# A hybrid recurrence and attention block on one core: the first value block by seven products, three projection blocks moved ahead of the recurrence, other places in the queues, and shorter shares of a pair

## The chip, the core and the metric

One core of one Trainium2 chip. The metric is device microseconds of one execution; the kernel before takes 1605.4 us, the median of three runs (1603.4 to 1609.9).

The engines are called by the names of the profile: PE is TensorE (PEld its weight loads), DVE is VectorE, ACT is ScalarE, POOL is GpSimd, SP is SyncE, which issues most loads. A "q" behind a name is that engine's queue, where its DMAs are issued.

## The reference, cut to what matters

```python
xn = rmsnorm(h, norm_gain) * (1 + scale) + shift        # 256 tokens; cn: 256 tokens of the context
aq, ak, av, ag, hq, hff, hfb, hi, hg, ma, mb = split_columns(xn @ w_in)      # w_in: 2048 x 19456
caq, cak, cav, cag, chq, chff, chfb, chi, chg, cma, cmb = split_columns(cn @ w_in)
q = rope(aq) * q_scale;  k = rope(ak)
att = window_attention(q, k, av, cak, cav, sink) * silu(ag)
# two gated recurrences over the tokens, forward and backward, 16 heads of 128 x 128,
# that start from the final states of the context
o, _, _ = hgrn2_bidir(to_heads(silu(hq)), to_heads(hi), k_f, g_f, k_b, g_b, s_f, s_b)
hgb = rmsnorm(o) * hgrn_norm_gain * silu(hg)
y = sigmoid(ma + b_merge[0]) * (hgb @ w_o_hgrn) + sigmoid(mb + b_merge[1]) * (att @ w_o_attn)
out = rmsnorm(h + gate * (y @ w_out)) * final_norm_gain
```

Everything is float32. The columns that both x and the context need are `hff` and `hfb` (forget gates), `hi` (values), `ak` and `av`. The others are needed for x alone.

## The kernel before

**Projections.** A float32 matrix product is made of three products of a coarser type: a weight chunk `raw` of 128 x 1024 (512 KB, loaded by SP, five buffers, `wload` L61) is split into `wh` (ACT, a copy, L78) and `wl` (DVE, raw minus wh, L79), three buffers of each; the activations lie split in `xHL`. High by high, low by high and high by low are summed in a PSUM bank (L93, L94, L96). The planner is told to put both halves of a split ahead of nearly everything else on their engines (`high_priority`). `proj_tok_g` (L101) makes 512 output columns for a list of token tiles in eight chunks; for two token tiles (x alone) that is 96 matmuls of 512 columns, for four (x and context) 192. `proj_col_x_g` (L140) makes 256 columns turned, with the weights as the moving or still side, for x alone.

**Seven products.** Where x and context are both wanted, `quad_tok` (L672) and `quad_col` (L624) treat tokens and columns as 2 x 2 blocks and make seven products of half size instead of eight, from sums of the tokens that `token_sums` (L555) makes once (the buffer `S`) and from sums of the weights (`combos`, L596, on DVE). A `quad_tok` of 512 columns is 336 matmuls of 256 columns (L717, L719, L722). Its results go to DRAM by POOL's queue (L727).

**Order of the stages.** (1) Modulation, and the first columns of the forget gates, up to 133 us. (2) The token stage: `proj_tok` of the first 512 value columns for four token tiles (`bv0`, L730); the two `token_sums` are made on DVE and ACT beside it; then `output_gate(0)` for x alone. (3) Three `quad_tok` of values, one of keys and one of attention values, and thirteen `quad_col` of forget gates, up to about 656 us. (4) The recurrence, eight pairs of heads, up to about 1252 us. (5) Attention together with `part_a` (`w_o_hgrn`), then `part_b` (`w_o_attn`), then `w_out`.

**The recurrence.** On PE the order is written by hand (`manual_schedule`): `weave` (L1028) lets `pair` (L781) run up to its next `yield` and then takes as much filler from `inputs` as that yield asks for, in units of 24 x 512 columns (`STEP`). The yields of a pair are its shares: 2.0, 0.5, 1.75, 4.0, 1.25 and 1.25 units. They lie between: turning of the context's forget gates (L919); `sb`, the state from the context (L936); the first levels (L856, after the copies of L829 and L832); the second levels (L856, after the products of L902), then `kt` (L962); `own` (L977), the pair's own contribution to the state; `S2` (L982, DVE), the state after half of the tokens; `ob` (L994 to L996), the output. The filler is the list `blocks` of `side_work` (L1158), 19 blocks of x alone in eight chunks of half a unit each, and at the end of each pair four chunks for the next pair's queries. `SIDE` (L1173) says how many items of the list fall to a pair: 20, the last pair 31. On the other engines the planner sets the order by its own model of time, except where `issue_after` queues an instruction behind a given one of the same engine.

Beside the filler run: `tasks_on` (L1082) at items 7, 10, 13 and 16 of a pair, which turns the attention's keys and queries: `attn_keys` (L1097) loads a tile `kr` from DRAM on POOL's queue, rotates it on DVE (`rope`, L1061, result `kx`) and is turned on PE at the next task (L1092); `load_forgets` (L1147), which loads the next pair's gates `F` by POOL and makes the context's decay by scans on DVE (`ctx_decay`, L765; L774, L778, L779); `gates` (L523), which sums 64 chunks `hgw` of `w_ada` into the output gate of the block, one chunk per 1.25 units of filler: a load of 256 KB into a single buffer (POOL, L526), one DVE instruction (L197), and after each sixteen chunks four transposes (L203). What is left of `gates` at the end is done by `run(gate)` (L1236). The results of the blocks go to DRAM: output gates `hg` (L521), rotated queries `qr` (L1133) and attention gates `ag` (L1145) by POOL's queue, merge gates (L1059) by ACT's. The small tiles `sm` have three buffers, `bb` two.

Of the kernel before, what the change touches and what calls it, by code (L numbers as in the profile page):

```python
# [7 lines left out]
F32 = mybir.dt.float32  # L8
# [30 lines left out]
def block_kernel(ctx: ExitStack, tc: tile.TileContext, x, c, cx, c_ctx, w_ada, b_ada, norm_gain, w_in,  # L39
# [29 lines left out]
    last_lo = [None]  # L69

    def wchunk(w, row0, nk, col0, ncol):
        cl = col0 if isinstance(col0, tuple) else (col0,)
        raw, rv = wload(w, row0, nk, cl, ncol)
        h = wp.tile([P, 1024], F32R, tag="wh", name="wh", bufs=3)
        lo = wp.tile([P, 1024], F32R, tag="wl", name="wl", bufs=3)
        n = len(cl) * nk * ncol
        with tc.high_priority(PRIO):
            act.activation(h[:, :n], raw[:, :n], AF.Copy)  # L78
            last_lo[0] = dve.tensor_tensor(lo[:, :n], raw[:, :n], h[:, :n].bitcast(F32), op=ALU.subtract).ins  # L79
        parts = [(h[:, g * nk * ncol: (g + 1) * nk * ncol].rearrange("p (k c) -> p k c", k=nk),  # L80
                  lo[:, g * nk * ncol: (g + 1) * nk * ncol].rearrange("p (k c) -> p k c", k=nk)) for g in range(len(cl))]
        return parts if isinstance(col0, tuple) else parts[0]
# [463 lines left out]
    with pl("sp", reuse_waits="tile") as sp:  # L546
# [182 lines left out]
        with tc.manual_schedule(engines={mybir.EngineType.PE}):  # L729
            bv0 = proj_tok(w_in, C_HI, x_st, range(4))  # L730
            for g in range(2):
                token_sums(g)
            for t in range(2):
                vo = fp.tile([P, 2, 512], F32, tag="F0", name="vo", bufs=2)
                with tc.high_priority(2 * PRIO):
                    act.activation(vo[:, 0, :], bv0[t], AF.Copy)
                    dve.tensor_copy(vo[:, 1, :], bv0[2 + t])
                nc.gpsimd.dma_start(v_dr[0][t], vo.rearrange("p a c -> p (a c)"))
            run(output_gate(0))
            for g in range(1, 4):  # L740
                quad_tok(C_HI + 512 * g, v_dr[g])
# [6 lines left out]

    def bias_row(row, n, late=None):
        bb = base.tile([P, 512], F32, tag="bb", name="bb", bufs=2)  # L750
        if late is not None:

            pool.tensor_copy(bb[:, 0:1], late)
        nc.gpsimd.dma_start(bb, row_bcast(b_merge[row: row + 1, n * 512: (n + 1) * 512], 512))
        return bb

# [24 lines left out]
    def pair(g, p, F, banks_q):  # L781
# [140 lines left out]
        yield 2.0  # L922
# [21 lines left out]
        yield 1.75  # L944
# [9 lines left out]
        yield 4.0  # L954
# [14 lines left out]
        yield 1.25  # L969
# [14 lines left out]
        yield 1.25  # L984
# [67 lines left out]
    def merge_out(row, n):  # L1052
        bb = bias_row(row, n)
        bm = yield from proj_tok_g(w_in, (C_MA, C_MB)[row] + n * 512, x_st, range(2))
        for t in range(2):
            sg = base.tile([P, 512], F32, tag="sm", name="sgm", bufs=3)
            dve.tensor_tensor(sg, bm[t], bb, op=ALU.add)
            act.activation(sg, sg, AF.Sigmoid)
            nc.scalar.dma_start((ma_dr, mb_dr)[row][n][:, t * 512: (t + 1) * 512], sg)  # L1059

# [19 lines left out]
    tasks, task = [], [None]  # L1080
# [16 lines left out]
    def attn_keys(z, t):  # L1097
        def fetch():
            kr = base.tile([P, 512], F32, tag="sm", name="kr", bufs=3)
            nc.gpsimd.dma_start(kr, kv_dr[0][t][:, z * 512: (z + 1) * 512])  # L1100
            if z == 0:
                kx, kr = kr, base.tile([P, 512], F32, tag="sm", name="kx", bufs=3)
                rope(kr.rearrange("p (r h d) -> p r h d", r=2, h=2), kx, t)
            return lambda: turn_tile(kr, [X[:, z: 8: 2, t * P: (t + 1) * P] for X in (XH, XL)])
        return fetch

    def attn_values():
        for t in range(4):
            vr = base.tile([P, 512], F32, tag="sm", name="vr", bufs=3)
            nc.gpsimd.dma_start(vr, kv_dr[1][t % 2][:, (t // 2) * 512: (t // 2 + 1) * 512])  # L1110
            rows = slice(8 + 2 * t, 10 + 2 * t)
            split(XH[:, rows, :], XL[:, rows, :], vr.rearrange("p (r c) -> p r c", r=2))
            yield

    def attn_queries(j):
# [14 lines left out]
        for t in range(2):  # L1130
            qr = base.tile([P, 512], F32, tag="sm", name="qr", bufs=3)
            rope(qr.rearrange("p (r h d) -> p r h d", r=2, h=2), bq[t], t)
            nc.gpsimd.dma_start(qr_dr[j][:, t * 512: (t + 1) * 512], qr)  # L1133
            tasks.append(lambda t=t: fetch(t))

    def attn_gates(j):
        for hf in range(2):
            bg = yield from proj_col_x_g(w_in, C_G + 512 * j + 256 * hf)
            for i, b in enumerate(bg):
# [5 lines left out]
                nc.gpsimd.dma_start(ag_dr[j][:, c0: c0 + T], sg)  # L1145

    def load_forgets(n):  # L1147
# [5 lines left out]
        for d in range(2):  # L1153
            ctx_decay(F, (d,))
# [3 lines left out]
    def side_work():  # L1158
        values = attn_values()
        tasks.extend(attn_keys(z, t) for z in range(2) for t in range(2))  # L1160
        blocks = (output_gate(1), merge_out(0, 0), output_gate(2), attn_queries(0), merge_out(0, 1), output_gate(3),
# [3 lines left out]
        for n, g in enumerate(blocks):  # L1165
            for k, got in enumerate(g):
                yield got
                if n > 16 and k % 2:
                    next(values, None)
            yield 0  # L1170

    side = side_work()
    SIDE = (20, 20, 20, 20, 20, 20, 20, 31)  # L1173
# [361 lines left out]
```

## Time and profile before

| | us |
|---|---|
| median of the runs (lowest, highest) | 1605.37 (1603.41, 1609.92) |
| the profiled execution | 1600.81 |
| its span, first to last instruction | 1599.0 |
| busy in the span: PE, PEld, DVE, ACT, POOL | 1570.7, 1343.6, 1182.7, 855.4, 157.6 |

The profile is of one execution. The span is what its rows add up to; 1.8 us of the execution lie around it. A PE row's length is partly modelled, so successive matmuls overlap in the rows: the distance between two starts is the pace of PE. `PEclk` is the granted TensorE clock as a share of 2.4 GHz; 0.5 is the lower of its two levels. A wait names the engine that came last before the waiting instruction could start.

### The profile page before, as it was taken

To read this page: it belongs to the slowest core of one execution; us is meant where nothing else is said; L and a number is where in the kernel's file an instruction comes from. 1 tells how busy PE (TensorE), PEld (TensorE's weight loads), DVE (VectorE), ACT (ScalarE), POOL (GpSimd) and SP (SyncE) were. 2 spreads that over 40 slices of the span, in tenths; PEclk is the share of its full clock that TensorE was granted. 3 is DMA by queue.
4 is the path that set the end of the run, shared out by engine and by line. 5 is a ranking of instruction groups with operands and counts; after the bars stand their busy time and mean duration, and the time that the engine had idled before them with its cause. 6 is when DMAs were issued, how large, how long until landed. Compare 5 with 4: busy or idle time off the path is not lost.

```text
span 1599.0 us, 27552 instructions
## 1 busy us (share of the span) xinstructions
PE 1570.7 (98%) x10810; PEld 1343.6 (84%) x10810; DVE 1182.7 (74%) x1745; ACT 855.4 (53%) x1338; POOL 157.6 (10%) x312
## 2 busy tenths in 40 slices
PE   7999999999999999999999999999999999999998
PEld 4567899999888888878888888788888888888887
DVE  4449677777888888786978887887977677757764
ACT  4334343333555555656566566565566776744442
POOL 2000000000000000111122222122112100000000
PEclk9999999999999999999999999999999999999999
DMA  9995533434444444776778787676788754558761
GB/s 368 386 386 175 160 120 127 138 130 129 148 134 132 132 132 132 250 235 219 234 251 282 248 266 240 223 263 218 249 275 277 254 160 157 158 172 281 231 209 69
DMA packets 238290, 333.81 MB, mean 209 GB/s; under 512 B 12080, under 2 KB 155856, under 8 KB 237392
## 3 DMA queue, kind: packets, MB, share of 16 engines
q1 hardware_dynamic: 212048, 249.54, 47.8%
q0 software_dynamic: 21216, 70.38, 12.8%
q10 hardware_dynamic: 4896, 12.13, 2.2%
q8 instruction: 85, 1.39, 0.4%
q14 instruction: 45, 0.37, 0.1%
HBM read 300.53 MB, written 31.47 MB: 208 GB/s over the span
## 4 chain that ended last, share of the span: by engine, by line
PE 90%; DMA 4%; DVE 3%; issue 2%; ACT 1%; SPq 0%; POOL 0%; POOLq 0%; DVEq 0%; ACTq 0%
PE pj L93 13%; PE pj L96 13%; PE pj L94 13%; PE pj L147 7%; PE pm L645 4%; PE pj L150 4%; PE pj L645 3%; PE pj L717 2%; PE pj L722 2%; PE pj L719 2%; PE pm L648 2%; PE pm L717 2%; PE pm L722 2%; PE pm L719 2%; PE pj L648 2%
## 5 line engine op out<-in xcount | busy, mean ns | idle before, releaser
L78 ACT ACTIVATE wh<-raw 128x1024 fp32r<-128x1024 f32 x292 | 307.2, 1059 | 262.3 <-PE pj L94 175.2
L79 DVE TENSOR_TENSOR wl<-raw,wh 128x1024 fp32r<-128x1024 f32 x292 | 354.8, 1222 | 125.3 <-ACT wh L78 121.5
L93 PE MATMUL pj<-wh,xHL 128*128 128x512 f32 (+1 forms) x832 | 326.2, 393 | 0.7 <-ACT sg L212 0.7
L94 PE MATMUL pj<-wh,xHL 128*128 128x512 f32 (+1 forms) x832 | 321.4, 388 | 0.0
L96 PE MATMUL pj<-wl,xHL 128*128 128x512 f32 (+1 forms) x832 | 219.7, 388 | 3.6 <-DVE wl L79 3.6
L93 PEld LDWEIGHTS pj<-wh,xHL 128*128 128x128 f32 x832 | 157.4, 189 | 33.1 <-ACT sg L212 1.9
L96 PEld LDWEIGHTS pj<-wl,xHL 128*128 128x128 f32 x832 | 154.6, 189 | 35.5 <-DVE wl L79 4.0
L94 PEld LDWEIGHTS pj<-wh,xHL 128*128 128x128 f32 x832 | 157.6, 189 | 30.2
L620 ACT ACTIVATE wh<-T 128x1024 fp32r<-128x1024 f32 x69 | 73.2, 1061 | 150.9 <-DVE T L601 75.5
L620 ACT ACTIVATE wh<-raw 128x1024 fp32r<-128x1024 f32 x92 | 96.8, 1054 | 62.2 <-PE pj L719 20.2
L147 PE MATMUL pj<-xHL,wh 128*128 128x512 f32 x512 | 129.9, 395 | 0.0
L621 DVE TENSOR_TENSOR wl<-raw,wh 128x1024 fp32r<-128x1024 f32 x92 | 112.1, 1219 | 7.4 <-ACT wh L620 7.3
L147 PEld LDWEIGHTS pj<-xHL,wh 128*128 128x128 f32 x512 | 92.5, 189 | 16.8
L621 DVE TENSOR_TENSOR wl<-T,wh 128x1024 fp32r<-128x1024 f32 x69 | 84.2, 1221 | 28.8 <-ACT wh L620 28.8
L150 PEld LDWEIGHTS pj<-xHL,wl 128*128 128x128 f32 x512 | 69.9, 190 | 5.5 <-issue 0.5
L150 PE MATMUL pj<-xHL,wl 128*128 128x256 f32 x512 | 71.6, 283 | 0.3 <-issue 0.3
L197 DVE SCALAR_TENSOR_TENSOR acc<-hgw,cg,acc 128x512 f32<-128x512 f32 x60 | 44.9, 749 | 29.6 <-DMA hgw<-in_w_ada_dram 29.5
L902 DVE TENSOR_TENSOR A<-A,X 128x512 f32<-128x512 f32 x96 | 61.9, 687 | 1.5 <-ACT Kmt L832 0.7
L526 POOL DMA_DIRECT2D hgw<-in_w_ada_dram x64 | 34.8, 544 | 263.8 <-DVE acc L197 210.0
L645 PE MATMUL pm<-S,wh 128*128 128x512 f32 x224 | 56.7, 395 | 0.8 <-ACT s L652 0.7
L601 DVE TENSOR_TENSOR T<-raw,T 128x1024 f32<-128x1024 f32 x46 | 56.1, 1219 | 0.0
L601 DVE TENSOR_TENSOR raw<-raw 128x1024 f32<-128x1024 f32 x23 | 28.2, 1225 | 35.3 <-DMA raw<-in_w_in_dram 35.3
(359 smaller groups left out, 3037.9 us busy)
## 6 DMA issues: line engine op xcount, KB each, us to landing
raw<-in_w_in_dram SPq DMA_DIRECT2D x300, 512.0 KB, 4.5
raw<-in_w_ada_dram SPq DMA_DIRECT2D x64, 512.0 KB, 8.0
hgw<-in_w_ada_dram POOLq DMA_DIRECT2D x64, 256.0 KB, 4.4
raw<-in_w_o_hgrn_dram SPq DMA_DIRECT2D x32, 512.0 KB, 3.6
raw<-in_w_o_attn_dram SPq DMA_DIRECT2D x32, 512.0 KB, 4.3
raw<-in_w_out_dram SPq DMA_DIRECT2D x28, 512.0 KB, 3.9
F<-F POOLq DMA_DIRECT2D x16, 512.0 KB, 6.6
F<-F ACTq DMA_DIRECT2D x13, 512.0 KB, 4.4
```

The costliest lines, as they stand in the source:

```text
L78: act.activation(h[:, :n], raw[:, :n], AF.Copy)
L79: last_lo[0] = dve.tensor_tensor(lo[:, :n], raw[:, :n], h[:, :n].bitcast(F32), op=ALU.subtract).ins
L93: pe.matmul(o, s[0], m[0], start=first, stop=False)
L94: pe.matmul(o, s[1], m[0], start=False, stop=False)
L96: pe.matmul(o, s[0], m[1], start=False, stop=last)
L147: pe.matmul(o.rearrange("p (a t) -> p a t", a=2), h[:, j, cs_], xHL[:, :, k0 + j, :T], start=k0 + j == 0, stop=False)
L150: pe.matmul(o[:, :T], lo[:, j, cs_], xH[:, k0 + j, :T], start=False, stop=k0 + j == KT - 1)
L601: dve.tensor_tensor(o, x_, y_, op=ALU.subtract)
L620: act.activation(h, src, AF.Copy)
L621: dve.tensor_tensor(lo, src, h.bitcast(F32), op=ALU.subtract)
L645: pe.matmul(m_[z].rearrange("p (z a t) -> p z a t", z=2, a=2), h[:, k, :], mv(k), start=fresh and k == 0, stop=False, skip_group_check=True)
L648: pe.matmul(pairs_of(m_[z][:, :T]), lo[:, k, :], mv(k)[:, 0], start=False, stop=k == 7, skip_group_check=True)
```

## The change

1. **Token stage.** The first value block is made by `quad_tok` like the other three. Beside the token sums stand `output_gate(0)`, `output_gate(1)`, `output_gate(2)` and `merge_out(0, 0)`, of which the last three leave the recurrence's list.
2. **Places in the queues.** `behind_chunk` queues what is traced within it behind the newest `wh` on ACT and the newest `wl` on DVE. It is put around `ctx_decay`, the rotation of keys, the splits of attention values and the sending of outputs. The rotation of a key tile becomes a task of its own, one after the load. Outputs of `output_gate`, `attn_queries` and `attn_gates` are collected in `outs` and sent by `send` on ACT's queue, in the recurrence one chunk later.
3. **Shares.** A pair's yields become 1.75, 0.5, 1.5, 3.5, 1.0 and 1.0 units, `SIDE` 17 for a pair and 25 for the last, for a list of 16 blocks. The pace of `gates` stays one chunk per 1.25 units.

```diff
-    last_lo = [None]
+    last_hi, last_lo = [None], [None]
+
+    def behind_chunk():
+        both = ExitStack()
+        both.enter_context(tc.issue_after(last_hi[0]))
+        both.enter_context(tc.issue_after(last_lo[0]))
+        return both
...
-            act.activation(h[:, :n], raw[:, :n], AF.Copy)
+            last_hi[0] = act.activation(h[:, :n], raw[:, :n], AF.Copy).ins
...
+    outs, tasks, task = [], [], [None]
+
+    def send():
+        while outs:
+            o = outs.pop(0)
+            nc.scalar.dma_start(*o[:2])
+            tasks.extend(o[2:])
...
-            nc.gpsimd.dma_start(hg_dr[g][:, t * 512: (t + 1) * 512], sg)
+            outs.append((hg_dr[g][:, t * 512: (t + 1) * 512], sg))
...
-            bv0 = proj_tok(w_in, C_HI, x_st, range(4))
-            for g in range(2):
-                token_sums(g)
-            for t in range(2):
-                vo = fp.tile([P, 2, 512], F32, tag="F0", name="vo", bufs=2)
-                with tc.high_priority(2 * PRIO):
-                    act.activation(vo[:, 0, :], bv0[t], AF.Copy)
-                    dve.tensor_copy(vo[:, 1, :], bv0[2 + t])
-                nc.gpsimd.dma_start(v_dr[0][t], vo.rearrange("p a c -> p (a c)"))
-            run(output_gate(0))
-            for g in range(1, 4):
+            for n, g in enumerate((output_gate(0), output_gate(1), output_gate(2), merge_out(0, 0))):
+                run(g)
+                send()
+                if n < 2:
+                    token_sums(n)
+            for g in range(4):
                 quad_tok(C_HI + 512 * g, v_dr[g])
...
-        yield 2.0
+        yield 1.75
...
-        yield 1.75
+        yield 1.5
...
-        yield 4.0
+        yield 3.5
...
-        yield 1.25
+        yield 1.0
...
-        yield 1.25
+        yield 1.0
...
-        if task[0]:
-            task[0]()
-        task[0] = tasks.pop(0)() if tasks else None
+        task[0] = (task[0]() if task[0] else None) or (tasks.pop(0)() if tasks else None)
...
-            if z == 0:
-                kx, kr = kr, base.tile([P, 512], F32, tag="sm", name="kx", bufs=3)
-                rope(kr.rearrange("p (r h d) -> p r h d", r=2, h=2), kx, t)
-            return lambda: turn_tile(kr, [X[:, z: 8: 2, t * P: (t + 1) * P] for X in (XH, XL)])
+            dst = [X[:, z: 8: 2, t * P: (t + 1) * P] for X in (XH, XL)]
+            if z:
+                return lambda: turn_tile(kr, dst)
+
+            def rotate():
+                kx = base.tile([P, 512], F32, tag="sm", name="kx", bufs=3)
+                with behind_chunk():
+                    rope(kx.rearrange("p (r h d) -> p r h d", r=2, h=2), kr, t)
+                return lambda: turn_tile(kx, dst)
+            return rotate
...
-            nc.gpsimd.dma_start(qr_dr[j][:, t * 512: (t + 1) * 512], qr)
-            tasks.append(lambda t=t: fetch(t))
+            outs.append((qr_dr[j][:, t * 512: (t + 1) * 512], qr, lambda t=t: fetch(t)))
...
-                nc.gpsimd.dma_start(ag_dr[j][:, c0: c0 + T], sg)
+                outs.append((ag_dr[j][:, c0: c0 + T], sg))
...
-            ctx_decay(F, (d,))
+            with behind_chunk() if last_lo[0] else ExitStack():
+                ctx_decay(F, (d,))
...
-        blocks = (output_gate(1), merge_out(0, 0), output_gate(2), attn_queries(0), merge_out(0, 1), output_gate(3),
+        blocks = (attn_queries(0), merge_out(0, 1), output_gate(3),
...
                 yield got
-                if n > 16 and k % 2:
+                if outs and k == 0:
+                    with behind_chunk():
+                        send()
+                if n > NB - 3:
                     next(values, None)
             yield 0
+        send()
...
-    SIDE = (20, 20, 20, 20, 20, 20, 20, 31)
+    SIDE = (17, 17, 17, 17, 17, 17, 17, 25)
```

## Rows read from the trace of the kernel before

**Rows 1.** The page: busy time of TensorE; the chain that ended last, by engine.
```profile
PE 1570.7 (98%) x10810; PEld 1343.6 (84%) x10810; DVE 1182.7 (74%) x1745; ACT 855.4 (53%) x1338; POOL 157.6 (10%) x312
...
PE 90%; DMA 4%; DVE 3%; issue 2%; ACT 1%; SPq 0%; POOL 0%; POOLq 0%; DVEq 0%; ACTq 0%
```

**Rows 2.** Waits of engine PE: us in total, times, longest us.
```profile
PE tkt L1092 <- DVE kx L1072: 3.9, 1, 3.9
PE pj L96 <- DVE wl L79: 3.6, 1, 3.6
```

**Rows 3.** Windows: length, then busy us (instructions) per engine, PEclk, DMA, GB/s.
```profile
132.70:199.50 66.80, 66.09 (x289) 53.76 (x289) 53.33 (x50) 28.81 (x32) 2.70 (x5) 1.00 0.48 157
...
177.60:199.50 21.90, 21.89 (x97) 18.02 (x97) 13.12 (x12) 7.91 (x8) 1.06 (x2) 1.00 0.67 214
199.58:239.90 40.32, 40.32 (x338) 40.31 (x337) 30.48 (x30) 16.53 (x18) 1.63 (x3) 1.00 0.37 120
```

**Rows 4.** Timeline of DVE in the first pair: start us, us, instruction, idle before.
```profile
706.23 0.69 DVE L1064 TENSOR_TENSOR kx<-kr,cs 128x512 f32<-128x512 f32 x1 [2.50 <-DMA kr<-kv]
```

**Rows 5.** Timeline of PE in the first pair.
```profile
710.68 1.09 PE L1092 MATMUL tkt<-cs,kx 128*128 128x128 f32 x4 [3.91 <-DVE kx L1072]
...
716.18 0.39 PE L93 MATMUL pj<-wh,xHL 128*128 128x512 f32 x1
```

**Rows 6.** Timeline of DVE in the fifth pair.
```profile
1000.96 0.69 DVE L778 TENSOR_TENSOR_SCAN e<-F,zero 128x255 f32<-128x255 f32 x1 [4.89 <-DMA F<-F]
...
1004.13 2.36 DVE L79 TENSOR_TENSOR wl<-raw,wh 128x1024 fp32r<-128x1024 f32 x2
```

**Rows 7.** Windows behind the two waits.
```profile
711.40:718.40 7.00, 7.00 (x24) 5.64 (x23) 6.47 (x10) 2.85 (x5) 1.20 (x4) 0.70 0.64 220
...
1005.40:1009.00 3.60, 3.60 (x9) 2.85 (x10) 3.60 (x5) 1.62 (x6) 0.00 (x0) 0.54 0.66 203
```

**Rows 8.** Groups of DVE, 816 to 888 us: count | busy us, mean ns | idle before.
```profile
L79 DVE TENSOR_TENSOR wl<-raw,wh 128x1024 fp32r<-128x1024 f32 x23 | 28.0, 1221 | 9.5 <-ACT wh L78 9.5
...
L1057 DVE TENSOR_TENSOR sgm<-pj,bb 128x512 f32<-128x512 f32 x2 | 1.3, 688 | 0.5 <-PE pj L96 0.5
```

**Rows 9.** Window of the second pair.
```profile
747.00:818.40 71.40, 71.12 (x606) 60.20 (x605) 58.27 (x94) 42.85 (x76) 13.84 (x27) 1.00 0.72 239
```

**Rows 10.** Timelines of ACT, PE, DVE and PE ahead of the two groups of levels.
```profile
1131.30 0.73 ACT L829 ACTIVATE F<-A 128x256 f32<-128x256 f32 x2 [2.78 <-DVE A L902]
...
1136.42 0.46 PE L856 MATMUL al<-qk 128*32 128x32 f32 x32
...
1011.91 1.29 DVE L902 TENSOR_TENSOR A<-A,X 128x512 f32<-128x512 f32 x2
...
1019.02 0.38 PE L856 MATMUL al<-Kmt 128*32 128x32 f32 x21
```

**Rows 11.** From `own` (L977) to `ob`: timelines of PE and DVE, chain of the last pair.
```profile
1096.57 1.16 PE L977 MATMUL al<-v,Kmt 128*128 128x128 f32 x8 [0.38 <-ACT X L868]
...
1103.00 1.12 DVE L982 SCALAR_TENSOR_TENSOR X<-so,X,al 128x128 f32<-128x128 f32 x4
...
1245.74 1.12 DVE L982 SCALAR_TENSOR_TENSOR X<-so,X,al 128x128 f32<-128x128 f32 x4
...
1240.73 1.83 PE pj L147 x8
...
1249.10 0.22 PE ob L994 x2
```

**Rows 12.** Timeline of ScalarE with its queue.
```profile
989.72 0.33 ACTq L1059 DMA_DIRECT2D ma<-sgm  x1
```

**Rows 13.** The gate chunks: transposes (L203), transfers (us to landing), waits of DVE.
```profile
L203 PE MATMUL tqg<-cs,acc x16: 270/273/276, 822.1 to 1218.3; 128*128 128x128 f32 x16
...
hgw<-in_w_ada_dram POOLq DMA_DIRECT2D x64, 256.0 KB, 4.4
...
DVE acc L197 <- DMA hgw<-in_w_ada_dram: 29.5, 17, 4.3
```

More of the change, by code (lines that the diff above doesn't have):

```diff
@@ L520, in output_gate, with bias_row, merge_out @@
             dve.tensor_tensor(sg, bg[t], sg, op=ALU.mult)
-            nc.gpsimd.dma_start(hg_dr[g][:, t * 512: (t + 1) * 512], sg)
+            outs.append((hg_dr[g][:, t * 512: (t + 1) * 512], sg))
+    def bias_row(row, n, late=None):
+        bb = base.tile([P, 512], F32, tag="bb", name="bb", bufs=2)
+        if late is not None:
+            pool.tensor_copy(bb[:, 0:1], late)
+        nc.gpsimd.dma_start(bb, row_bcast(b_merge[row: row + 1, n * 512: (n + 1) * 512], 512))
+        return bb
+    def merge_out(row, n):
+        bb = bias_row(row, n)
+        bm = yield from proj_tok_g(w_in, (C_MA, C_MB)[row] + n * 512, x_st, range(2))
+        for t in range(2):
+            sg = base.tile([P, 512], F32, tag="sm", name="sgm", bufs=3)
+            dve.tensor_tensor(sg, bm[t], bb, op=ALU.add)
+            act.activation(sg, sg, AF.Sigmoid)
+            nc.scalar.dma_start((ma_dr, mb_dr)[row][n][:, t * 512: (t + 1) * 512], sg)
     def gates():
@@ L747, in block_kernel @@
                         quad_col(d, 2 * n)
[L749 to L755, printed above, removed]
     hp = ctx.enter_context(pl("hg", reuse_waits="tile"))
@@ L1050, in load_values @@
         nc.gpsimd.dma_start(hg, hg_dr[g].rearrange("p (t c) -> p t c", t=2)[:, :, cl])
[L1052 to L1059, printed above, removed]
     def rope(dst, src, t):
@@ L1078, in split @@
         dve.tensor_tensor(dl, src, dh.bitcast(F32), op=ALU.subtract)
-    tasks, task = [], [None]
     def tasks_on():
-        if task[0]:
-            task[0]()
-        task[0] = tasks.pop(0)() if tasks else None
+        task[0] = (task[0]() if task[0] else None) or (tasks.pop(0)() if tasks else None)
     def turn_tile(src, dst, scale=1.0):
@@ L1110, in attn_values @@
             nc.gpsimd.dma_start(vr, kv_dr[1][t % 2][:, (t // 2) * 512: (t // 2 + 1) * 512])
+            yield
             rows = slice(8 + 2 * t, 10 + 2 * t)
-            split(XH[:, rows, :], XL[:, rows, :], vr.rearrange("p (r c) -> p r c", r=2))
+            with behind_chunk():
+                split(XH[:, rows, :], XL[:, rows, :], vr.rearrange("p (r c) -> p r c", r=2))
             yield
@@ L1132, in attn_queries @@
             rope(qr.rearrange("p (r h d) -> p r h d", r=2, h=2), bq[t], t)
-            nc.gpsimd.dma_start(qr_dr[j][:, t * 512: (t + 1) * 512], qr)
-            tasks.append(lambda t=t: fetch(t))
+            outs.append((qr_dr[j][:, t * 512: (t + 1) * 512], qr, lambda t=t: fetch(t)))
     def attn_gates(j):
         for hf in range(2):
-            bg = yield from proj_col_x_g(w_in, C_G + 512 * j + 256 * hf)
+            cols_ = proj_col_x_g(w_in, C_G + 512 * j + 256 * hf)
+            for k in range(4):
+                yield next(cols_)
+                if k == 0 and outs:
+                    with behind_chunk():
+                        send()
+            bg = result(cols_)
             for i, b in enumerate(bg):
@@ L1167, in side_work @@
                 yield got
-                if n > 16 and k % 2:
+                if outs and k == 0:
+                    with behind_chunk():
+                        send()
+                if n > NB - 3:
                     next(values, None)
             yield 0
+        send()
     side = side_work()
-    SIDE = (20, 20, 20, 20, 20, 20, 20, 31)
+    SIDE = (17, 17, 17, 17, 17, 17, 17, 25)
     def inputs(n, res):
```

2 lines of the change are left out of this document (1 added, 1 removed).

## The prediction, made before the changed kernel was run

> **What bounds the kernel now.** I began with the page: TensorE (PE) is busy for 1570.7 of 1599.0 us and carries 90% of the chain that ended last [rows 1]. A busy PE need not be a fast one, so I then looked for places where PE waits, and for places where it runs below its usual pace. The table of PE's waits has two of size after the opening: once 3.9 us for the rotated keys `kx`, once 3.6 us for the low half `wl` of a weight chunk [rows 2]. The windows by stage show what an undisturbed stage looks like: a block of two token tiles (97 records of 512 columns) takes 21.9 us, a seven-product block of value columns (338 records of 256 columns) 40.3 us, PE without a gap in both [rows 3]. So PE is the bound nearly everywhere, and a change can win in three ways only: less PE work, no PE waits, no slow clock.
>
> Both waits have one cause. VectorE (DVE) works its queue off in order, and an instruction that waits for a DMA holds up what is queued behind it. In the first pair the rotation of `kx` starts after 2.50 us of idle, ended by the DMA of `kr` [rows 4]; the transposes of `kx` start only at 710.68, and PE has those four and the next twelve matmuls behind it only at 716.18 [rows 5]. In the fifth pair a scan of `ctx_decay` starts after 4.89 us of idle, ended by the DMA of `F`; the two `wl` behind it follow at 1004.13 [rows 6]. Behind each wait the granted clock is down, to means of 0.70 and 0.54, so it stood at its lower level, 1.2 GHz, for a part of the stretch: 24 matmuls take 7.0 us, 9 take 3.6 us [rows 7], where 0.226 us each is usual [rows 3].
>
> **The change, part by part.** The sum is made against the profiled execution, 1600.8 us (span 1599.0). The median of the runs shown, 1605.4, lies 4.6 above it; I add these 4.6 at the end, having no reason to expect another distance.
>
> *Value block by seven products.* Out go 192 matmuls of 512 columns, two blocks of 96 at 21.75 us [rows 3]: 43.5 us. In come 336 of 256 columns: 40.3 us, as in the block shown (four more of the same line follow it without a wait in rows 2). On PE: -3.2 us. Its extra combinations and splits, some 1.22 us each, lie on DVE, which is busy for 30.5 of the 40.3 us while PE has no gap [rows 3]. Uncovered, one late `wl` would cost what rows 2 show, 3.6 us.
>
> The Trainium skill speaks against this part ("TensorE: Matmul & The Clock Gate", section "Part 3: Packing small matmuls"): a weight load overlaps running matmuls only where the row groups differ, so 336 loads would cost more than 192. By that page's rate for a load (128 columns at 1.2 per ns) the block would take some 12 us more instead of 3.2 less, an estimate. The trace does not agree: loads fill 40.3 us beside matmuls that fill the same 40.3 us.
>
> *Three blocks moved.* `output_gate(1)`, `merge_out(0, 0)` and `output_gate(2)` keep their 3 x 21.75 us of PE. Their 24 weight loads on SP come one per chunk of 2.7 us beside the token sums, where a block of this kind moved 214 GB/s and PE did not wait [rows 3]; a bias row goes to POOL and six outputs to ScalarE's queue. `send` puts these behind a product of DVE, so the next `wh` on ScalarE can wait there for about an instruction. DVE, busy for 53.3 of 66.8 us in the old stage [rows 3], gets 16 more `wl` of 1.22 us and six outputs of 0.69 us [rows 8]: 77 of 87 us, crowded but below PE. I cost the move at nothing; three buffers of `wh` and `wl`, two chunks ahead, cover it. Without that cover one wait like those above would come, some 4 us.
>
> *Stalls.* The rotation of the keys now runs a task later than its DMA is issued, and `ctx_decay` is queued behind the newest chunk. I take both waits as gone: 3.9 us [rows 2] and 2.4 us of slow pace (710.68 to 716.18 is 5.5 us for what needs 3.1) [rows 5] in the first pair, 3.6 us [rows 2] and 1.6 us (3.6 less 9 x 0.226) [rows 7] in the fifth: -6.3 and -5.2. The other end is no gain, if the late transfer holds DVE at its new place too.
>
> *Shorter shares.* Counting the yields against chunks of 0.5 units, a pair gets 2.0, 0.5, 2.0, 4.0, 1.0, 1.5 units of filler before, and 2.0, 0.5, 1.5, 3.5, 1.0, 1.0 after; a pair of 71.4 us [rows 9] becomes one of about 63. So PE comes one chunk (2.8 us) earlier to three places: the first levels, the second levels, and `ob`. At the first levels the tightest pair has 4.4 us between ScalarE's last copy (ends 1132.03) and PE's read (1136.42), at the second 5.8 us (1013.20 to 1019.02) [rows 10]; both stay positive. At `ob` the state update on L982 decides. `own` ends at 1097.73 and at 1240.73 in the two latest pairs; L982 ends 6.4 and 6.1 us later; PE reaches `ob` at 1249.10, three chunks and 8.4 us after `own` [rows 11]. After two chunks, 5.6 us, PE would wait 0.8 and 0.5 us. With some slow clock behind: +2 us. Bounds: 0, and 22 us if every pair waits a whole chunk.
>
> *Output DMAs.* Those of gates and queries leave POOL's queue for ScalarE's; an issue there takes 0.33 us [rows 12], 32 make 11 us, on an engine busy for 42.9 of 71.4 us in a pair [rows 9]. They are queued behind a later chunk, so their data is ready. I cost them at nothing; bounds 0 and one late `wh` or `wl`, 4 us. Their `sm` buffers are held a chunk longer; the next `kr` on POOL or `e` on DVE would wait for that.
>
> *Gate chunks.* `gates()` needs 67 turns (64 chunks), one per 1.25 units. Before, the fillers make 90 units, 72 turns, and its last column transposes run at 1218.2, within the recurrence. After, 78 units make 62 turns. Three chunks and the generator's end fall to `run(gate)` at the start of attention, where no edge ties them to a chunk. Each waits for a transfer of 4.4 us, and DVE has stood up to 4.3 us for one [rows 13]. PE needs none of them, but a `wl` behind them can be late: +2 us; bounds 0 and 13 (3 x 4.3).
>
> Sum: -3.2 - 6.3 - 5.2 + 2 + 2 = -10.7, so 1590.1 for a profiled execution and **1594.7 us** for the median.
>
> **Rivals.**
> A. The DMA waits go on elsewhere. DVE still waits for `hgw`, 17 times and 29.5 us in all [rows 13], and for `kr`. Two PE waits per run of the size seen put 11.5 us back: 1606.2. For: DVE is busy for four fifths of a pair [rows 9] and in order. Against: the edges name just the instructions that did it.
> B. Slower: the shares are too short. If DVE's new order puts two more `wl` in front of L982 in every pair, it ends 8.4 us after `own`; PE then waits 2.8 us at `ob` in all eight pairs and by the ratio seen (11.5 lost for 7.5 waited) loses 4.3 each: 34 us in place of the 2, so 1626.7. It decides from about 1.7 us of waiting per pair (20.7 us lost in all). For: the least distance before is 2.0 us [rows 11]; against: in the other six pairs L982 ends earlier.
> C. The gate tail is dear: three transfers one after the other, 4.4 us each and 0.75 of DVE, stand in DVE's and POOL's queues at the first scores; if 10 of these 15 us reach PE, 8 more than my 2: 1602.7.
> D. Weight loads are bare: 144 more of them at 0.12 us each, 17.3 us, in place of the 3.2 gained: 1615.2. The block of rows 3 is evidence against it.
>
> **How the numbers follow.** A measurement of this kernel tells about 0.5%, 8 us: faster is below 1597.3, slower above 1613.4. Forecast 0.60, of it 0.55 faster; its own range is 1585 to 1600 (nothing added by shares or gate tail: 1590.7; the 4.6 us of run spread gone as well: 1586). A 0.17, nearly all of it the same. B 0.12, slower. C 0.09, the same, a little of it faster. D 0.02, slower. Faster 0.57, same 0.29, slower 0.14. The range takes in A and C, 1585 to 1609; outside lie B, D and the ends of the others, near 0.2.
>
> **What would show it.** Right: no PE wait for `kx`, none for `wl` above 1 us; a granted clock of 1.00 through the recurrence; a value block of 40.3 us in place of the four-tile block; pairs of about 63 us; waits at `ob` below 1 us. Wrong: new lines of PE waits on `ob` or on the levels in most pairs; DVE idle before `kr`, `F` or `hgw` and PE waiting for `wl` behind it; a gap of PE near the first scores. A recurrence that is shorter by no more than the three blocks it gave away makes the forecast wrong, even if the value block gains its 3.2 us.

## The result and the profile after

The change makes the kernel a little slower: 1611.17 us in the median (1608.48 to 1614.89), beside 1604.03 us of the kernel before on the same chips; ratio 1.004 [1.003, 1.005]. The profiled execution has a span of 1606.8 us in place of 1599.0, 7.8 more. The forecast was 10.7 less, so some 18 us have to be explained.

The page, PE's busy time and the chain by engine, as in [rows 1]:

```profile
PE 1568.8 (98%) x10954; PEld 1348.8 (84%) x10954; DVE 1202.7 (75%) x1764; ACT 861.4 (54%) x1344; POOL 139.8 (9%) x280
...
PE 90%; DMA 3%; DVE 3%; issue 2%; ACT 1%; SPq 0%; POOL 0%; POOLq 0%; DVEq 0%; ACTq 0%
```

PE is busy for 1.9 us less and the span is 7.8 us longer: the time went into waits. The table of PE's waits after the opening (us in total, times, longest), beside [rows 2]:

```profile
PE tqg L210 <- DVE bL L1038: 4.7, 1, 4.7
PE kt L980 <- DVE A L920: 3.7, 1, 3.7
PE pj L100 <- DVE hsum L165: 2.5, 1, 2.5
...
PE tkt L1097 <- DVE redg L212: 1.9, 1, 1.9
PE tgr L572 <- DVE gcol L214: 1.7, 1, 1.7
PE al L874 <- ACT so L850: 1.5, 1, 1.5
...
PE tkt L1097 <- DVE kx L1081: 0.2, 1, 0.2
```

The two old waits are gone (`kx` is left with 0.2 us, `wl` is not among them), and seven new ones of 1 us or more stand in their place (the seventh, of 1.0 us, is shown at the start of attention), all on DVE or on what DVE feeds. In the changed kernel the levels stand at L874, the products ahead of them (`grow`) at L920, `kt` at L980, the gate chunk at L204 and its transposes at L210. The windows of the token stage, the first value block, the first, second and sixth pair (length, busy per engine PE, PEld, DVE, ACT, POOL, then PEclk, DMA share, GB/s), beside [rows 3, 9]:

```profile
133.60:220.40 86.80, 86.80 (x384) 71.81 (x383) 73.10 (x70) 46.39 (x51) 1.61 (x3) 1.00 0.69 223
220.40:260.70 40.30, 40.30 (x337) 40.26 (x337) 30.83 (x31) 16.56 (x18) 0.53 (x1) 1.00 0.39 127
729.80:802.20 72.40, 67.00 (x579) 56.28 (x578) 55.88 (x91) 38.61 (x69) 10.53 (x23) 0.98 0.70 229
802.20:871.30 69.10, 66.08 (x582) 55.66 (x581) 56.09 (x91) 41.75 (x71) 11.74 (x24) 0.98 0.71 234
1064.40:1126.90 62.50, 62.50 (x582) 53.88 (x581) 51.86 (x86) 39.46 (x74) 9.81 (x21) 1.00 0.75 244
```

The token stage with its four blocks and the value block have no gap of PE. The sixth pair is 62.5 us long, as forecast; the first is 72.4 and the second 69.1, with the same count of matmuls (579 and 582). Pairs counted from their first `tw` transposes to the next pair's: 77.6, 71.4, 71.8, 72.2, 73.2, 72.9, 70.6 before; 72.3, 69.2, 66.7, 62.4, 63.9, 62.5, 64.0 after.

**The first pair.** PE's timeline (start, us, instruction, idle before), the two places where it waits:

```profile
778.40 0.65 PE L874 MATMUL al<-so,acc 128*32 128x64 f32 x32 [1.49 <-ACT so L850]
...
782.72 1.29 PE L980 MATMUL kt<-cs,A 128*128 128x128 f32 x4 [3.66 <-DVE A L920]
```

DVE's timeline ahead of the second:

```profile
775.88 1.29 DVE L920 TENSOR_TENSOR A<-A,X 128x512 f32<-128x512 f32 x2
777.08 0.69 DVE L1081 TENSOR_TENSOR kx<-kx,rt 128x512 f32<-128x512 f32 x1
777.68 1.26 DVE L796 TENSOR_TENSOR_SCAN e<-F,zero 128x255 f32<-128x255 f32 x2
778.86 2.34 DVE L86 TENSOR_TENSOR wl<-raw,wh 128x1024 fp32r<-128x1024 f32 x2
781.11 0.75 DVE L204 SCALAR_TENSOR_TENSOR acc<-hgw,cg,acc 128x512 f32<-128x512 f32 x1
781.97 1.29 DVE L920 TENSOR_TENSOR A<-A,X 128x512 f32<-128x512 f32 x2
```

DVE doesn't idle here. The last step of `grow` (L920) starts at 781.97, behind the end of the second key rotation (L1081), two scans, two `wl` and a gate chunk. The granted clock right after is 0.73:

```profile
783.50:787.50 4.00, 4.00 (x15) 3.28 (x15) 0.57 (x2) 3.35 (x11) 0.00 (x0) 0.73 0.49 174
```

With that, the two waits cost about 6.9 us.

**The start of the second pair.** PE's timeline:

```profile
805.70 0.50 PE L100 MATMUL pj<-wh,xHL 128*128 128x512 f32 x1 [2.50 <-DVE hsum L165]
```

A share of 17 items is nine of one block (eight chunks, then the item that reads its two PSUM banks out) and eight of the next, so the first pair stops between a block's last chunk and its read-out. The next pair's queries, made at the end of each pair, hold the other two of the four `pj` banks. So the next block has no bank until DVE comes to the sums of the queries (`hsum`, from 805.23); the finished block's own read-out (`sgm`) follows at 806.81 and 808.61. The clock behind the wait:

```profile
806.00:809.50 3.50, 3.50 (x10) 2.68 (x9) 3.16 (x6) 1.41 (x4) 0.18 (x1) 0.52 0.68 247
```

This costs about 4.3 us. Two smaller waits, of 0.5 us near 859 and of 1.9 us near 893, add 2.4; in the second the turned queries (`tkt`) wait until DVE has read the gate's transposes (`redg`) out of the only bank of the tag `tp`.

**The start of attention.** PE's timeline, the windows of the stretch (columns as above) and DVE's timeline:

```profile
1274.14 1.08 PE L210 MATMUL tqg<-cs,acc 128*128 128x128 f32 x4 [4.70 <-DVE bL L1038]
...
1276.91 0.37 PE L572 MATMUL tgr<-cs,gcol 128*16 128x128 f32 x1 [1.69 <-DVE gcol L214]
...
1278.30 0.80 PE L92 MATMUL sc<-xHL,qTa 128*128 128x512 f32 x1 [1.02 <-ACT pr L1309]
```

```profile
1268.00:1275.00 7.00, 2.30 (x11) 1.56 (x9) 5.67 (x13) 5.56 (x8) 0.54 (x1) 0.91 0.99 320
1275.00:1285.00 10.00, 7.29 (x21) 5.36 (x20) 4.16 (x13) 6.46 (x14) 1.05 (x2) 0.55 0.34 119
```

```profile
1256.94 0.75 DVE L204 SCALAR_TENSOR_TENSOR acc<-hgw,cg,acc 128x512 f32<-128x512 f32 x1 [2.25 <-DMA hgw<-in_w_ada_dram]
...
1263.01 0.75 DVE L204 SCALAR_TENSOR_TENSOR acc<-hgw,cg,acc 128x512 f32<-128x512 f32 x1 [1.85 <-DMA hgw<-in_w_ada_dram]
...
1267.11 0.75 DVE L204 SCALAR_TENSOR_TENSOR acc<-hgw,cg,acc 128x512 f32<-128x512 f32 x1 [1.27 <-DMA hgw<-in_w_ada_dram]
...
1273.51 0.48 DVE L1038 SCALAR_TENSOR_TENSOR bL<-to,cols,bH 128x256 fp32r<-128x256 f32 x1
```

The last gate chunks wait for their transfers one behind the other, 5.4 us of DVE in all. The last `bL`, which reads the only bank of the tag `tp`, comes at 1273.51, and the gate's own transposes `tqg` need that bank. PE stands for 4.7, 1.7 and 1.0 us, and ten microseconds behind have a granted clock of 0.55, so mostly the lower level, 1.2 GHz. Against full pace this stretch loses 9.5 us; before, 0.9.

The sum of the terms: -4.6 (value block, 44.9 to 40.3 us), -11.5 (old waits), +6.9, +4.3, +2.4 (first pairs), +8.6 (start of attention) = +6.1; the span says +7.8. The 1.7 us between are not assigned.

### The profile page after: what moved, and what is told of

Read it like the earlier page. It is cut to its first block, busy times and chain, and to the rows that moved or that the text cites. A ratio compares the mean times of both kernels' runs of the same rounds, so it can differ in the third digit from the quotient of the medians.

```text
span 1606.8 us, 27861 instructions
## 1 busy us (share of the span) xinstructions
PE 1568.8 (98%) x10954; PEld 1348.8 (84%) x10954; DVE 1202.7 (75%) x1764; ACT 861.4 (54%) x1344; POOL 139.8 (9%) x280
## 3 DMA queue, kind: packets, MB, share of 16 engines
q0 software_dynamic: 19168, 64.08, 11.5%
## 4 chain that ended last, share of the span: by engine, by line
PE 90%; DMA 3%; DVE 3%; issue 2%; ACT 1%; SPq 0%; POOL 0%; POOLq 0%; DVEq 0%; ACTq 0%
PE pj L100 13%; PE pj L101 12%; PE pj L103 12%; PE pj L154 7%; PE pj L677 5%; PE pm L677 4%; PE pj L157 3%; PE pj L754 3%; PE pj L751 3%; PE pj L749 3%; PE pm L754 2%; PE pm L751 2%; PE pm L749 2%; PE pj L680 2%; PE pm L680 2%
## 5 line engine op out<-in xcount | busy, mean ns | idle before, releaser
L100 PE MATMUL pj<-wh,xHL 128*128 128x512 f32 (+1 forms) x768 | 299.8, 392 | 2.5 <-DVE hsum L165 2.5
L101 PE MATMUL pj<-wh,xHL 128*128 128x512 f32 (+1 forms) x768 | 296.1, 387 | 0.0
L103 PE MATMUL pj<-wl,xHL 128*128 128x512 f32 (+1 forms) x768 | 203.0, 386 | 0.0
L100 PEld LDWEIGHTS pj<-wh,xHL 128*128 128x128 f32 x768 | 145.1, 189 | 31.4 <-DVE hsum L165 2.7
L652 ACT ACTIVATE wh<-T 128x1024 fp32r<-128x1024 f32 x75 | 79.5, 1061 | 171.4 <-DVE T L633 82.6
L101 PEld LDWEIGHTS pj<-wh,xHL 128*128 128x128 f32 x768 | 145.2, 189 | 27.9
L103 PEld LDWEIGHTS pj<-wl,xHL 128*128 128x128 f32 x768 | 142.4, 188 | 29.1
L653 DVE TENSOR_TENSOR wl<-T,wh 128x1024 fp32r<-128x1024 f32 x75 | 91.5, 1220 | 32.1 <-ACT wh L652 32.1
L920 DVE TENSOR_TENSOR A<-A,X 128x512 f32<-128x512 f32 x96 | 61.8, 684 | 1.9 <-ACT Kmt L850 1.2
L633 DVE TENSOR_TENSOR T<-raw,T 128x1024 f32<-128x1024 f32 x50 | 60.9, 1218 | 0.0
L204 DVE SCALAR_TENSOR_TENSOR acc<-hgw,cg,acc 128x512 f32<-128x512 f32 x60 | 44.7, 745 | 17.2 <-DMA hgw<-in_w_ada_dram 17.1
L677 PE MATMUL pj<-S,wh 128*128 128x512 f32 x208 | 52.5, 394 | 0.8 <-ACT s L684 0.8
```

The costliest lines, as they stand in the source:

```text
L100: pe.matmul(o, s[0], m[0], start=first, stop=False)
L101: pe.matmul(o, s[1], m[0], start=False, stop=False)
L103: pe.matmul(o, s[0], m[1], start=False, stop=last)
L633: dve.tensor_tensor(o, x_, y_, op=ALU.subtract)
L652: act.activation(h, src, AF.Copy)
L653: dve.tensor_tensor(lo, src, h.bitcast(F32), op=ALU.subtract)
```

## Experiments

Each ratio is to runs of the kernel before that were taken beside it.

**The gate tail.** Theory: chunks that fall to the start of attention cost there what was lost. Rival: turned back into the recurrence, they crowd DVE there. Edit, to 1.1 units a turn:

```diff
-            if count[0] >= 1.25 * STEP:
-                count[0] -= 1.25 * STEP
+            if count[0] >= 1.1 * STEP:
+                count[0] -= 1.1 * STEP
```

> The changed kernel with the gate chunks taken every 1.1 units of filler instead of 1.25, so that 70 turns fit and none of the 67 is left for the start of attention. Theory (gate tail): in the changed kernel PE loses 4.7 us before the last column transposes and 1.7 us before the row transposes at 1269 to 1277 us, and some 3 us by a clock at 0.5 behind them; all of it goes, -8 to -9 us against the changed kernel, a span near 1598 and 0.4 to 0.6% faster than the changed kernel, about equal to the kernel before. Rival (short tail): with 1.5 units behind the last output instead of 2.5, turned outputs and first scores come late whatever the gates do; then PE still waits 4 us or more at the start of attention and no more than 2 us are gained. Second rival (crowding): seven more gate chunks, 0.75 us each on DVE, within the pairs make other instructions late there, and 3 to 5 us come back as waits in the pairs.

Measured: 1616.18 us, 1.0053 [1.0034, 1.0072]. The tail goes, but the crowding, which the expectation priced at 3 to 5 us, is dearer than what it saves: the start of attention loses 3.2 us in place of 9.5, and PE's loss within the recurrence rises from 23.2 to 36.8 us. PE's waits, DVE's wait for the gate transfers, and the seventh pair (64.0 us in the changed kernel):

```profile
PE kt L980 <- DVE A L920: 3.2, 2, 3.0
...
DVE acc L204 <- DMA hgw<-in_w_ada_dram: 28.0, 21, 5.3
...
1133.00:1206.50 73.50, 67.36 (x584) 56.52 (x583) 57.80 (x96) 39.19 (x73) 15.71 (x29) 0.95 0.73 243
```

In the changed kernel the wait for `hgw` is 17.1 us in 14 times. The gate work can't be had for nothing at either place.

**The ordering alone, and the change without it.** The kernel before gets `last_hi`, `behind_chunk`, `outs` and `send`, the rotation as a task of its own, and the edges on `ctx_decay` and on the split of the values; stages, shares and value block stay old:

```diff
+                with behind_chunk():
+                    rope(kx.rearrange("p (r h d) -> p r h d", r=2, h=2), kr, t)
...
-            ctx_decay(F, (d,))
+            with behind_chunk() if last_lo[0] else ExitStack():
+                ctx_decay(F, (d,))
...
-            nc.gpsimd.dma_start(qr_dr[j][:, t * 512: (t + 1) * 512], qr)
+            outs.append((qr_dr[j][:, t * 512: (t + 1) * 512], qr, lambda t=t: fetch(t)))
```

> The kernel before with the other places in the queues alone (edges behind a chunk, the rotation as a task of its own, outputs on ScalarE's queue); value block, list of blocks and shares as before. Theory (the prediction's step): the waits of 3.9 us for the rotated keys and of 3.6 us for a late low half go, with their slow clock: -11.5 us, 0.993 of the kernel before. Rival (waits move): DVE is as crowded and the DMA waits only stand elsewhere; PE waits of 5 us or more appear at other lines of the first pair or before a chunk, and the ratio is 0.997 to 1.003.

Measured: 1596.66 us, 0.9935 [0.9917, 0.9953], some 10.4 us less; the -11.5 of the prediction lies within the interval. The second kernel takes the same lines out of the changed one; the outputs of gates and queries go by POOL's queue again, and `send` is left with nothing to send:

> The changed kernel without the other places in the queues (value block by seven products, moved blocks and shorter shares kept). Theory (shares and gate tail cost, edges help): the wait for rotated keys in the first pair and one for a late low half come back, and the gate tail stays; 3 to 8 us slower than the changed kernel. Rival (the edges themselves cost): the waits in the first pair at the second levels and at the bank of the next block go with the edges, and it is 5 us or more faster than the changed kernel.

Measured: 1611.31 us, 1.0027 [1.0011, 1.0043]. That is the changed kernel's time, neither of the two numbers expected. PE's waits:

```profile
PE tkt L1099 <- DVE kx L1081: 4.1, 1, 4.1
PE pj L100 <- DVE hsum L165: 2.5, 1, 2.5
...
PE tgr L572 <- DVE gcol L214: 2.2, 1, 2.2
PE tkt L1099 <- DMA qr<-qr: 2.1, 1, 2.1
```

The wait for `kx` is back, and the one ahead of `kt` is gone (`tqg` is left with 0.7 us). So the edges do what they say in both kernels; with the shorter pairs, what they save at one place is lost at others.

**Longer shares in the first pair**, beside the 1.1 units of the first experiment:

```diff
-        yield 3.5
+        yield 4.0 if h0 == 0 else 3.5
...
-    SIDE = (17, 17, 17, 17, 17, 17, 17, 25)
+    SIDE = (20, 17, 17, 17, 17, 17, 17, 22)
```

(and 2.0, 1.75, 1.25, 1.25 at the other yields of the first pair).

> As the run with a gate chunk per 1.1 units, and the first pair keeps its old shares (2.0, 0.5, 1.75, 4.0, 1.25, 1.25 units, 20 items; the last pair 22). Theory (the first pair alone is too crowded for short shares, since the key rotations fall into it): the waits of 1.5 us at the second levels and 3.7 us before the transposes of the keys' decay go, with some 1.5 us of slow clock, and the wait of 2.5 us for a bank behind that pair moves or goes: 5 to 9 us less than the run with the pace alone, span 1589 to 1594. Rival: DVE is late in the first pair by more than a chunk whatever the share, or the wait turns up at the next pair; less than 2 us are gained.

Measured: 1609.3 us, 1.0025 [1.0008, 1.0041], 0.28% below the first experiment. That is less than the 5 to 9 us of the theory and more than the rival's 2. In the first pair the wait at the second levels is gone and the one ahead of `kt` is down to 2.0 us, but other places have new waits, and the start of attention loses 9.9 us:

```profile
PE to L1032 <- DVE so L1024: 3.0, 1, 3.0
PE sc L92 <- DMA qTa<-q: 2.3, 1, 2.3
```

The short shares are not the whole of the first pair's loss. The window of the first pair here, then with the ordering alone, which has the same shares:

```profile
730.10:807.20 77.10, 71.42 (x601) 59.65 (x600) 62.28 (x99) 40.64 (x65) 9.91 (x22) 1.00 0.74 235
```

```profile
671.80:743.40 71.60, 70.77 (x603) 59.67 (x602) 57.95 (x90) 41.53 (x67) 8.87 (x21) 1.00 0.77 247
```

Here the pair is 5.5 us longer and DVE busy for 4.3 us more. Two things differ besides the earlier stages: the gates' pace, and the list of blocks. With three blocks moved, `attn_queries(0)` is the first block of the pair, and its rotation too falls to DVE there (754.3 to 760.4 us in the changed kernel), shortly before `grow` and the key rotations. No run varies the list alone, so this part of the loss is not divided.

**Two blocks moved in place of three.** `merge_out(0, 0)` goes back into the recurrence, the fourth yield is 4.0 again, and the gate's turns come every 1.2 units, enough for 68:

```diff
-            for n, g in enumerate((output_gate(0), output_gate(1), output_gate(2), merge_out(0, 0))):
+            for n, g in enumerate((output_gate(0), output_gate(1), output_gate(2))):
...
-        yield 3.5
+        yield 4.0
...
-    SIDE = (17, 17, 17, 17, 17, 17, 17, 25)
+    SIDE = (18, 18, 18, 18, 18, 18, 18, 27)
...
-            if count[0] >= 1.25 * STEP:
+            if count[0] >= 1.2 * STEP:
```

> A version meant to beat both kernels: the changed kernel with two blocks moved instead of three (the first merge gate stays in the recurrence), second-level share 4.0 units, 18 items per pair and a gate chunk per 1.2 units, so that 82 units make 68 turns and none is left for attention. Theory (the places in the queues give -10 us as the run with them alone showed, the value block -3 to -5, and a pair of 10 units with all turns within it is long enough): 1590 to 1595, 0.988 to 0.994 of the kernel before. Rival (DVE is too full for anything shorter than the old pair): the first pair loses 5 us or more and the whole is no better than the places in the queues alone, 0.994 to 1.004.

Measured: 1591.28 us, 0.9918 [0.9894, 0.9941]: the lowest of all, below both kernels. Its interval overlaps that of the ordering alone, 0.9935 [0.9917, 0.9953]. PE's longest wait after the opening, and the window of the first seven pairs and most of the eighth:

```profile
PE al L995 <- ACT X L886: 1.8, 1, 1.8
...
707.70:1250.20 542.50, 536.84 (x4804) 459.75 (x4802) 451.32 (x745) 337.68 (x614) 104.82 (x206) 1.00 0.78 254
```

A granted clock of 1.00 through the recurrence is what the prediction had asked of the changed kernel. One block of 21.7 us at another place, half a unit more in a pair, shares of 18 items and gates that end within the recurrence are together worth 1.2% against the changed kernel.

**The suspected costs one by one**, in the changed kernel. The rotation of the keys left out:

```diff
-            if z:
+            if z < 2:
                 return lambda: turn_tile(kr, dst)
```

> The changed kernel with the rotation of the two key tiles left out (the attention's keys of the first half of the heads are then not rotated; eight DVE instructions, 4.4 us, less in the first pair, and one task each less). Theory (the rotations crowd DVE in the first pair): the waits of 1.5 us at the second levels and 3.7 us before the decay's transposes go, with their slow clock; 4 to 8 us less than the changed kernel. Rival (shares too short for the first pair anyway, scans and copies being late): PE waits at the second levels stay above 3 us, and less than 3 us are gained.

Measured: 1604.24 us, 0.9995 [0.9983, 1.0006], some 7 us below the changed kernel. The wait ahead of `kt` falls from 3.7 to 1.8 us and the one at the second levels is gone; the other two places stay:

```profile
PE tqg L210 <- DVE bL L1038: 4.3, 1, 4.3
...
PE pj L100 <- DVE hsum L165: 2.5, 1, 2.5
PE kt L980 <- DVE A L920: 1.8, 2, 1.6
```

One item more in the first share (18, 17 x 6, 24):

> The changed kernel with one item more in the first pair (18, and 24 in the last), so that the first pair no longer ends exactly where a block's last chunk ends. Theory (the wait of 2.5 us for a bank behind the first pair, found with the same length in all runs with 17 items, comes from that: the next block needs a bank at once, while the queries still hold two and the finished block two): it goes, with some 1.5 us of slow clock; 3 to 5 us less than the changed kernel. Rival (the wait for the sums of the queries is DVE's lateness, not the banks' meeting): the wait stays or comes back as another one, and nothing is gained.

Measured: 1607.47 us, 1.0018 [1.0003, 1.0033]. The wait for the bank stands at the end of the second pair, PE's timeline:

```profile
873.41 0.79 PE L100 MATMUL pj<-wh,xHL 128*128 128x512 f32 x1 [2.49 <-DVE hsum L165]
```

18 + 17 items are 35, three blocks and eight items, so now the second pair stops ahead of a block's read-out. The wait follows that split, as in the run with longer first shares, where the fourth pair ends so (71 items) and the next starts with 2.2 us of it. The end of a block alone does not make it: with 18 items throughout (the kernel with two blocks moved) every pair ends with a block and its read-out, and none starts with such a wait. Nor is the split always enough: in the kernel before the fourth pair ends at 80 items, eight blocks and eight items, but DVE had read that block's banks at 950.79, ahead of the sums of the queries, and PE starts the next block at 963.26 without a wait. The edit does not remove the wait, so the 3.5 us gained are not its price; in the profiled executions the gain is 1.3 us, with 3.3 us of wait for `tqg` in place of 4.7.

The last five of the 64 gate chunks left out, so that the generator ends within the recurrence:

```diff
-            for k0 in range(KT):
+            for k0 in range(KT if g < 3 else KT - 5):
...
-                if (g, k0) != (3, KT - 1):
+                if (g, k0) != (3, KT - 6):
```

> The changed kernel with the last five of the 64 gate chunks left out (the output gate of the last 512 columns then lacks 640 of its 2048 terms), so that 62 turns are enough at the old pace and nothing of the gates stands at the start of attention. Theory (gate tail): the 4.7 and 1.7 us waits at the start of attention and their slow clock go, 7 to 9 us less than the changed kernel, about 1.000 of the kernel before or a little under. Rival (short tail): some 4 us of waits for turned outputs, queries or scores stay at the start of attention, and 4 us or less are gained.

Measured: 1603.18 us, 0.9994 [0.9980, 1.0009], some 7 to 8 us below the changed kernel. `tqg` and `tgr` wait no more; at the start of attention 2.3 us are left:

```profile
PE kt L980 <- DVE A L920: 3.7, 1, 3.7
...
PE sc L92 <- ACT pr L1309: 2.3, 1, 2.3
```

All three at once (no rotation, 59 chunks, shares 16, 17 x 5, 18, 25, where no pair stops ahead of a read-out):

> The changed kernel with three causes taken out together: the rotation of the two key tiles left out, the last five gate chunks left out, and the items of the pairs as 16, 17 (five times), 18, 25, so that no pair ends with a block's last chunk (with 18 in the first pair the second one ended so, and the wait for a bank came there). Theory (the three causes are the whole loss and add up, 7 + 8 + 4 us): 1590 to 1594, 0.990 to 0.995 of the kernel before, and no wait of PE above 2 us in the recurrence. Rival (DVE's order is redrawn by each edit and other waits of the same size take their place): 1598 or more, with new lines of waits.

Measured: 1598.24 us, 0.9964 [0.9945, 0.9982]. By the medians that is 12.9 us below the changed kernel (by the ratios 12.2), where 7, 7.5 and the 3 to 5 expected of the share add to 18 or more. It is the rival's number (1598 or more). The wait for a bank at a pair's start is gone, but two of about 2 us stay, at `kt` and at the scores, where the changed kernel waits 1.0:

```profile
PE kt L980 <- DVE A L920: 2.4, 2, 2.2
PE sc L92 <- ACT pr L1309: 2.3, 1, 2.3
```

The gate tail and the rotations are shown each by a run without them, the bank by the split that it follows and by its absence here; together they are worth less than their sum. Where the distance of some 7 us to the kernel with two blocks moved lies (which does all of the work), these runs don't settle.

**The parts within the best kernel.** First, its first value block by four tiles and 192 matmuls, as before:

```diff
-            for g in range(4):
+            bv0 = proj_tok(w_in, C_HI, x_st, range(4))
...
+            for g in range(1, 4):
                 quad_tok(C_HI + 512 * g, v_dr[g])
```

> The version with two moved blocks, its first value block made again for four token tiles at once (192 matmuls of 512 columns, one product after another) in place of seven products. Theory (PE's work counts, 43.5 us against 40.3): 3 us slower than that version, at most 5. Rival (the seven products cost other engines as much as they save PE): within 1 us of it.

Measured: 1599.72 us, 0.9976 [0.9962, 0.9990], some 8 us above that version, more than the 5 expected. The window of the block in this kernel, then in the one with seven products:

```profile
198.10:243.40 45.30, 44.09 (x193) 35.66 (x192) 15.82 (x15) 10.43 (x13) 0.00 (x0) 1.00 0.33 104
```

```profile
198.10:238.41 40.31, 40.31 (x337) 40.31 (x336) 29.73 (x30) 16.64 (x18) 0.53 (x1) 1.00 0.39 125
```

The block itself is 5.0 us longer: 3.8 of PE's work and 1.2 of a wait for a bank. A further 2.2 us lie in the first pair, which the edit does not touch: its wait at `own` is 2.1 us in place of 1.8, and the 5.8 us behind it have a granted clock of 0.71 in place of 1.00.

Second, the best kernel without its ordering:

> The version with two moved blocks without the other places in the queues. Theory (the edges and the later rotation are worth their 10 us here too): the wait of some 4 us for rotated keys in the first pair and one or two others come back, 6 to 12 us slower than that version. Rival (with two blocks moved and the gates within the recurrence the order matters little, as in the run that took the edges from the changed kernel and found no loss): within 3 us of it.

Measured: 1605.54 us, 1.0003 [0.9984, 1.0021], some 14 us above the best kernel. PE's waits:

```profile
PE tkt L1099 <- DMA qr<-qr: 6.7, 3, 3.0
PE tkt L1099 <- DVE kx L1081: 3.0, 1, 3.0
```

Here the ordering is worth at least as much as alone.

The last two runs also price the moved blocks and short shares. With the ordering but without seven products they measure 0.9976 [0.9962, 0.9990], where the ordering alone measures 0.9935 [0.9917, 0.9953]: some 6.5 us slower. Without the ordering, seven products and two moved blocks are no faster than the kernel before (1.0003), though the value block saves 4.6 to 5.0 us. So the moved blocks, the shorter shares and the faster gate pace together gain nothing in either comparison; they cost some 5 us. The ordering and the seven products with all blocks in their old places, by the sum about 15 us less than the kernel before (an estimate from -10.4 and -4.6), was not run.

## Why the prediction was wrong

- **Value block, -3.2: right in kind, 1.4 us too small.** 40.30 us, PE without a gap. Loads fill 40.26 us beside matmuls that fill 40.30, so rival D falls. The old block was priced by two blocks of 21.75, but the windows of [rows 3] give it 44.9 (66.80 less 21.90), so it is worth -4.6; beside the moved blocks the old block costs 5.0 more.
- **Three blocks moved at nothing: right at their place.** Four blocks in 86.80 us at full pace; DVE busy 73.1 us, 77 forecast. The sum has no term for what the move does to the list: `attn_queries(0)` with its rotation becomes the first block of the first pair.
- **Stalls, -6.3 and -5.2: right alone, worth nothing in sum here.** Both waits are gone, and the ordering alone measures -10.4 us. But the changed kernel has the same time without it. The prediction weighed rival A as DMA waits that move on elsewhere; what came are mostly waits for DVE's own queue.
- **Shorter shares, +2: the step that failed first, by 11.6 us.** The first three pairs measured 13.6 (6.9 + 4.3 + 2.4). The prediction looked for the loss at `ob` in every pair, with rival B as the dear end. No pair waits there, and pairs four to seven take 62.4 to 64.0 us, about the 63 forecast. The step that failed is the slack at the second levels: 5.8 us in the tightest pair [rows 10], said to "stay positive" when PE comes 2.8 us earlier. That slack was read in a pair without key rotations; in the first pair the two rotations, which the change itself places behind a chunk, stand in front of `grow` (without them the time is 7 us less). How much of the first pair's loss is the shares' own and how much the list's and the gates' stays open: with the old shares there, at the faster gate pace, it still took 77.1 us, where the ordering alone took 71.6. And no step of mine counted items against blocks, by which 17 = 9 + 8 stops a pair ahead of a block's read-out: the experiment on the share moved that wait with the count.
- **Gate chunks, +2: mis-sized by 6.6 us.** The count of turns, 62 for 67, was right, and so was the place. It measured +8.6, within the bounds of 0 and 13, and by rival C's mechanism, which I priced at 10 of 15 us reaching PE and gave 0.09. I had argued that PE needs none of the chunks; it needs the bank that the transposes behind them share with `turned`.
- **Output DMAs at nothing: right.** No wait of the changed kernel is for them; in the best kernel without the ordering PE waits 6.7 us for `qr`. That is no rule, though: in the profile of the ordering alone, an execution of 1600.57 us and the longest of that kernel, PE waited once for 6.3 us for `qr`, with the output DMA behind a chunk.

Together: the forecast of -10.7, with 11.6 and 6.6 added and 1.4 taken off, gives +6.1 of the +7.8.

## What to carry to other kernels

Shortening the fill between dependent steps takes slack from every place of the pipeline at once, so look for the place with most other work in the in-order queue (here the first pair with the one-time rotations), not for the pair with the least slack on average. When items are dealt out in shares, count whether a share stops between a block's last product and the item that frees its banks, and when work runs over its stage's end, look at which buffers the stage behind shares with it. A removed stall pays only as long as PE still has slack at the next late instruction: the ordering gave 0.65% alone and nothing beside the shorter pairs of the changed kernel. And test each part of a change by itself: here the ordering and the value block carry the gain, and the moved blocks, shorter shares and gate pace none of it.

## What the runs showed that I had not expected

In the changed kernel the PE waits of 2.5 to 4.7 us are followed by 3 to 10 us at a granted clock of 0.52 to 0.73, which costs some 1.5 to 2 us more each. Effects taken out one by one (7 us for the rotations, 7.5 for the gate tail) and the split of the shares give 12 together, and waits of about 2 us stay in that run; the same ordering is worth 10.4 us in the kernel before, nothing in the changed one, and 14 us in the one with two blocks moved.
